# Four buffers for kept products, a second queue for finished rows and no first burst of weight differences in a decoder-layer kernel

## The chip, the core and the metric

The kernel runs on one core of a Trainium2 chip. A core has TensorE (PE, matrix products into PSUM banks), VectorE (DVE) and ScalarE (ACT) for element-wise work, GpSimd (POOL) for some element-wise work, and SyncE (SP), which here only issues transfers. Transfers between the chip's memory (HBM) and the on-chip memory (SBUF) run on 16 DMA engines; an instruction on SP, ACT or POOL asks for one, and each of these engines issues in the order of its own instructions, so a transfer that must wait holds up what stands behind it. The metric is the device time of one execution in microseconds (us); times are the median of several runs.

## The reference

One decoder layer on 2048 tokens of width 1024, in float32:

```python
hn = rms_norm(h, mix_pre_g)
proj = hn @ w_in                       # q, k, v and the input of a convolution group
attn_out = sliding_window_attention(q, k, v, attn_sinks, rel_bias)
conv_out = conformer_conv(u, conv_dw, conv_dw_b, conv_ln_g, conv_ln_b, w_conv_pw)
mixed = jnp.concatenate([attn_out, conv_out], axis=-1) @ w_out
h = h + rms_norm(mixed, mix_post_g)
hn = rms_norm(h, ffn_pre_g)
ff = (jax.nn.silu(hn @ w_gate) * (hn @ w_up)) @ w_down      # w_down: 2816 x 1024
h = h + rms_norm(ff, ffn_post_g)
```

## The kernel before

Tokens are worked on in four tiles of 512, numbered 0 to 3. Every float32 operand is split into a rounded high part and a low part (ScalarE copies the high part, `split_f` at line 840; VectorE or GpSimd subtracts, `lo` at line 844), and every product is made of three TensorE products: high by high, high by low, low by high. A matmul instruction multiplies a 128x128 block by 128x512 into one PSUM bank.

The name of a buffer in the profile is its tag, an @ and the stage: A are the input projections, B attention, C the convolution, W the output projection, H the preparation of the hidden rows for the feed-forward part, F the feed-forward products with w_gate and w_up, G the down projection with w_down. The feed-forward part takes two token tiles as one pair: tiles 0 and 1 are the first pair (stages H0, F0, G0 in the code), tiles 2 and 3 the second (H2, F2, G2). The page leaves the digits out.

For a pair, each product with w_gate and w_up is a 2x2 block product that is made with seven half-size products instead of eight, from sums and differences of the blocks of hidden rows and of the weights. The stage F has two parts.

- The early part, `stage_pre`, line 921, needs only plain blocks of hidden rows. It runs for PRE weight columns (20 for the first pair, 16 for the second). In its first half it makes the product of A11 and B11 for each of them, copies it out of its bank (line 983) and writes it to HBM (`keeps`, line 980): these are the kept results. In its second half it fetches a kept result (`fetch`, line 939, into a tile with the tag `gb`, asked for at line 943), copies it into a free PSUM bank with ScalarE (`seed`, line 955, the copy at 959) and adds the product of A12 and B21 on top. That is one block of the result, and it goes through silu (line 988) and the product of the two halves to HBM (`mids`, line 991). Weights are loaded two products at a time into `raw` (line 936).
- The main part, `stage_p1`, line 997, makes the other products. It needs sums of hidden rows, which `stage_h_sums` (line 882, operations at 893 and 904) makes while the early part runs, and fetches the kept results once more (line 1043).

A product has 12 matmuls. There are four PSUM banks for products, two buffers for `gb`, two for `at`, three for `fc`, one for `wx` and five for `chl` (`BUFS`, line 53).

The down projection (`stage_p2`, line 1163) is also made with seven products. It needs differences of the blocks of w_down; `stage_tsums` (line 1119) makes them once, during the main part of the first pair: for each of 11 groups GpSimd's queue loads four blocks (line 1126), VectorE makes four differences, and GpSimd's queue writes each to HBM (`td`, line 1138). When the four row blocks of a pair are done, `finish` (line 1141) normalises them: it reads the rows of h from `h_scr` into `chl` (line 1155), VectorE multiplies and adds, and the finished rows are written to `out` (line 1159). For the first pair this falls into the early part of the second.

The order of the work: the main line of stages is run by `run` (line 1399), and each of its yields gives so many us of estimated time to a set of lanes (`Lane`, line 1320). A lane holds stages that go on beside the main line; it earns credit at its rate, capped at 6.0, and while it has credit its next piece is emitted. A lane without work also earns. The differences of w_down are on the lane `lt` with the rate 0.2; a group costs 3.9 for its loads and 0.25 for each difference. The framework then sets the order of each engine's instructions by priorities in order of emission and by its own estimate of when an instruction could start; a difference is also tied to the newest matmul, so that it does not stand far ahead of the products.

Of the kernel before, what the change touches and what calls it, by code (L numbers as in the profile page):

```python
# [37 lines left out]
def layer_kernel(ctx, tc, x, xT, cols, rows, sinks, relb, onehot, w_in, w_pw, w_out, w_gate, w_up, w_down, out):  # L38
# [22 lines left out]
    def f2(tag, shape=(P, T)):  # L61
        return t_(tag, shape)
# [111 lines left out]
    def after_first(first, r, how="NoSync"):  # L174
        tc.add_manual_dep(
            r.ins,
            first.ins.name,
            mybir.DependencyInfo(getattr(mybir.DependencyClass, how), mybir.DependencyReason.DATA),
            reason="products of half the array stand together",
        )  # L180

    def three(o, pairs, first=True, last=True):
        n = 3 * len(pairs)
# [737 lines left out]
    def stage_pre(ws, ops, mid, keep, q0=0, q1=None):  # L921
        PRE = PRES[ws[0]]
        q1 = q1 or 2 * PRE
        L = f"F{ws[0]}"
        raws = {}
        wops = {}
        kept = {}

        def load(q):
            if q < q1 and q % 2 == 0:  # L930
                lab[0] = L
                half, m = divmod(q, PRE)
                raw = t_("raw", (P, 2, T))
                for j in range(2):
                    src, pr = MATS[m + j]
                    nc.sync.dma_start(raw[:, j], src[2 * pr][:, half * T : (half + 1) * T])
                    raws[q + j] = raw[:, j]

        def fetch(q):
            if PRE <= q < q1:  # L940
                lab[0] = L
                kept[q] = f2("gb")
                nc.sync.dma_start(kept[q], keep[q - PRE])

        def split(q):
            if q < q1:
                lab[0] = L
                raw = raws.pop(q)
                wops[q] = split_f(raw, hl("w"))
                lo(raw, wops[q], False)  # L950

        seeded = {}
        pend = []

        def seed(q):
            if PRE <= q < q1:
                lab[0] = L
                seeded[q] = mm()
                act(seeded[q], kept.pop(q), AF.Copy)  # L959

        load(q0)
        load(q0 + 2)
        for q in range(q0, q0 + 3):
            split(q)
        for q in range(q0, q1):
            half, m = divmod(q, PRE)
            started.add(f"P{ws[0]}.{q}")
            bn = "B21" if half else "B11"
            if len(ops.get(bn, ())) < 4:
                lh.until(f"{bn}.{ws[0]}")  # L970
            split(q + 3)
            load(q + 4)
            fetch(q + 2)
            lab[0] = L
            seed(q + 1)
            lab[0] = L
            o = seeded.pop(q) if half else mm()
            product(o, wops.pop(q), ops[bn], not half)
            while pend:
                nc.sync.dma_start(*pend.pop())  # L980
            if not half:
                u = f2("fa")
                act(u, o, AF.Copy)
                pend.append((keep[m], u))
            else:
                if MATS[m][0] is w_gate:
                    sg = f2("fa")
                    act(sg, o, AF.Silu)
                else:
                    vtt(sg, sg, o, ALU.mult)  # L990
                    nc.sync.dma_start(mid[0, MATS[m][1]], sg)
            yield 2.76
        while pend:
            lab[0] = L
            nc.sync.dma_start(*pend.pop())
# [123 lines left out]
    def stage_tsums(td):  # L1119
        L = "G0"  # L1120
        for pr in range(NF // 2):
# [6 lines left out]
            b11, b12, b21, b22 = b  # L1128
            for to, o, p_, q_ in ((0, b11, b12, b11), (2, b12, b22, b12), (1, b22, b22, b11), (3, b21, b21, b22)):
                lab[0] = L  # L1130
                r = vtt(o, p_, q_, ALU.subtract)
                tc.add_manual_dep(
                    r.ins,
                    made["rows"][-1].name,
                    mybir.DependencyInfo(mybir.DependencyClass.NoSync, mybir.DependencyReason.DATA),
                    reason="weight differences keep pace with the products",
                )
                nc.gpsimd.dma_start(td[to, pr], o)
                yield 0.25

    def finish(L, gb, jobs, pool=True):
        lab[0] = L
        n_ = len(jobs)
        ssq = sm(4)
        for j, (rows_, halves) in enumerate(jobs):
# [6 lines left out]
        r = rsqrt(ssq[:, 0:n_], n_, 1, pool)  # L1152
        for j, (rows_, halves) in enumerate(jobs):
            ht = f4("chl" if L == "G0" else "mid")
            nc.sync.dma_start(ht, h_scr[rows_])
            for n in range(2):
                cs = slice(n * T, (n + 1) * T)
                stt(halves[n], halves[n], r[:, j : j + 1], ht[:, cs], ALU.mult, ALU.add)
                nc.sync.dma_start(out[rows_, cs], halves[n])
            yield 2.0  # L1160
            lab[0] = L

# [304 lines left out]
    del normed[:]  # L1467
    lh.add("S0", stage_h_sums(ws, ops), lambda: "N1" in lh.done)
    run(stage_pre(ws, ops, mids[0], keeps[0], Q0))
    lt.add("TS", stage_tsums(td))  # L1470
    run(stage_p1(ws, ops, mids[0], keeps[0]))
    lt.until("TS")
# [80 lines left out]
```

## Time and profile before

| | |
|---|---|
| three runs, us | 1948.69, 1951.76, 1952.41 (median 1951.76) |
| the profiled execution: its own time, its span, us | 1951.41, 1949.7 |
| TensorE busy, us and share of the span | 1902.9, 98% |
| VectorE, ScalarE, GpSimd busy, share | 76%, 49%, 15% |
| mean granted TensorE clock | 0.993 |
| early part, first pair and second pair, us from the start, about | 498 to 650, 1286 to 1396 |
| main part, first and second pair, about | 650 to 980, 1396 to 1725 |

The profile is one execution. A line such as `PE mm@F L85 <- ACT mm@F L959: 13.6, 7, 5.1` says that TensorE stood idle before instructions of line 85 that write `mm@F`, until the ScalarE instruction of line 959 was done: 13.6 us in total, 7 times, 5.1 us the longest. In a timeline a row gives the start, the length, the engine, the line, the operation, what it writes and reads, how many in a row, and in brackets the idle time ahead and what ended it. "SPq" is SP issuing a transfer, and "DMA x<-y" is a transfer in flight. A table of stretches gives for each stretch the busy time of each engine with the number of instructions, then the mean granted clock, the share of the 16 DMA engines' time and GB/s. Line 85 is the helper that emits every matmul and line 94 the one that emits every VectorE operation, so the names of the buffers tell which stage a row belongs to.

### The profile page before, as it was taken

Reading aid. Unit: us, or ns where it says so; the run is one execution under the profiler, and the core shown is the slowest. Engines: PE = TensorE matmul, PEld = TensorE weight load, DVE = VectorE, ACT = ScalarE, POOL = GpSimd, SP = SyncE. Lnnn points to the kernel's source line nnn. Section 1 sums busy time; section 2 is a strip of 40 time slices with the busy share of each in tenths; the row PEclk is TensorE's granted clock in tenths of the full one; section 3 lists DMA queues with packets and bytes.
Section 4 is the critical chain, followed back from the end, with each engine's and each line's share of the span. In section 5 each row is a group of like instructions: output and inputs, shape, how many; then the busy total and the mean of one; then the engine's idle time right before and its main releaser. Section 6 shows DMA issues by size and latency. Waiting matters only on the chain.

```text
span 1949.7 us, 26646 instructions
## 1 busy us (share of the span) xinstructions
PE 1902.9 (98%) x8730; PEld 1537.4 (79%) x8730; DVE 1475.9 (76%) x2648; ACT 958.6 (49%) x1886; POOL 299.0 (15%) x427
## 2 busy tenths in 40 slices
PE   8999999999999999999999999998999999999997
PEld 6777777777777787788888788886788888888886
DVE  4999979995986998888579945578677776465557
ACT  5355455457658433334353555476534333345453
POOL 4011021011120111120000100000032333211003
PEclk9999999999999999999999999998999999999998
DMA  8787667667758767676477876769645443375663
GB/s 308 250 309 229 220 209 236 199 206 237 245 199 288 269 227 257 241 269 228 144 272 240 315 249 206 237 235 362 216 159 162 154 154 103 124 252 185 206 199 141
DMA packets 209578, 435.67 MB, mean 223 GB/s; under 512 B 21752, under 2 KB 39328, under 8 KB 209440
## 3 DMA queue, kind: packets, MB, share of 16 engines
q1 hardware_dynamic: 191648, 402.52, 61.8%
q0 software_dynamic: 7040, 23.07, 3.4%
q10 hardware_dynamic: 10752, 8.39, 1.3%
q8 instruction: 68, 1.11, 0.2%
q14 instruction: 70, 0.57, 0.1%
HBM read 323.26 MB, written 110.63 MB: 223 GB/s over the span
## 4 chain that ended last, share of the span: by engine, by line
PE 67%; DVE 15%; DMA 10%; issue 4%; ACT 2%; POOL 2%; SPq 1%; DVEq 0%; POOLq 0%; ACTq 0%
PE mm@F L85 30%; PE mm@G L85 17%; PE mm@A L85 8%; DVE fc@C L94 5%; PE mm@W L85 4%; PE tr@W L85 3%; PE tr@B L85 2%; DMA mids<-fa@F 2%; DVE w@F L94 1%; DMA keeps<-fa@F 1%; DVE chl@F L94 1%; DVE fa@F L94 1%; DMA w@W<-fold 1%; DMA gb@F<-keeps 1%; PE tr@B L504 1%
## 5 line engine op out<-in xcount | busy, mean ns | idle before, releaser
L94 DVE SCALAR_TENSOR_TENSOR fc@C<-glu@C,colt,fc@C 128x512 f32<-128x512 f32 x480 | 359.0, 762 | 2.7
L85 PE MATMUL mm@F<-hl@H,w@F 128*128 128x512 f32 x1056 | 261.1, 398 | 14.8 <-ACT mm@F L959 13.6
L85 PEld LDWEIGHTS mm@F<-hl@H,w@F 128*128 128x128 f32 x1056 | 201.1, 192 | 61.6 <-ACT mm@F L959 17.7
L85 PE MATMUL mm@G<-hl@G,hl@G 128*128 128x512 f32 x924 | 227.4, 393 | 1.8 <-DVE hl@G L94 1.8
L841 ACT ACTIVATE w@F<-chl@F 128x512 fp32r<-128x512 f32 x220 | 136.3, 626 | 186.3 <-PE mm@F L85 164.8
L85 PE MATMUL mm@A<-hl@A,w@A 128*128 128x512 f32 x840 | 207.9, 395 | 4.0 <-ACT w@A L127 2.1
L85 PEld LDWEIGHTS mm@G<-hl@G,hl@G 128*128 128x128 f32 x924 | 171.6, 188 | 38.3 <-DVE hl@G L94 2.6
L85 PE MATMUL mm@G<-w@G,hl@G 128*128 128x512 f32 x876 | 199.4, 389 | 0.0
L94 DVE TENSOR_TENSOR w@F<-chl@F,w@F 128x512 fp32r<-128x512 f32 x198 | 151.0, 765 | 59.9 <-ACT w@F L841 59.7
L85 PEld LDWEIGHTS mm@G<-w@G,hl@G 128*128 128x128 f32 x876 | 164.5, 188 | 34.1
L85 PEld LDWEIGHTS mm@A<-hl@A,w@A 128*128 128x128 f32 x840 | 155.2, 188 | 43.2 <-issue 3.9
L85 PE MATMUL mm@F<-mid@H,w@F 128*128 128x512 f32 x528 | 132.7, 392 | 0.8 <-DVE fa@F L94 0.8
L85 PE MATMUL mm@F<-ql@H,w@F 128*128 128x512 f32 x528 | 130.1, 391 | 0.7 <-ACT w@F L841 0.7
L85 PE MATMUL mm@F<-p@H,w@F 128*128 128x512 f32 x528 | 129.1, 389 | 0.0
L85 PE MATMUL mm@F<-x@H,w@F 128*128 128x512 f32 x528 | 125.7, 391 | 0.0
L85 PEld LDWEIGHTS mm@F<-mid@H,w@F 128*128 128x128 f32 x528 | 99.8, 189 | 22.3 <-ACT at@F L1086 1.2
L85 PEld LDWEIGHTS mm@F<-x@H,w@F 128*128 128x128 f32 x528 | 98.7, 188 | 21.3 <-issue 0.8
L85 PEld LDWEIGHTS mm@F<-p@H,w@F 128*128 128x128 f32 x528 | 99.1, 188 | 20.6
L85 PEld LDWEIGHTS mm@F<-ql@H,w@F 128*128 128x128 f32 x528 | 98.5, 188 | 21.1 <-ACT w@F L841 1.1
L507 POOL TENSOR_SCALAR_AFFINE_SELECT p@B<-p@B 128x512 f32<-128x512 f32 x62 | 56.6, 918 | 338.1 <-ACT p@B L505 336.6
L127 ACT ACTIVATE w@A<-raw@A 128x512 fp32r<-128x512 f32 x110 | 67.4, 626 | 82.4 <-PE mm@A L85 50.3
L94 DVE TENSOR_TENSOR w@G<-raw@G,w@G 128x512 fp32r<-128x512 f32 x73 | 53.6, 734 | 71.7 <-ACT w@G L841 70.7
(316 smaller groups left out, 3240.0 us busy)
## 6 DMA issues: line engine op xcount, KB each, us to landing
mids<-fa@F SPq DMA_DIRECT2D x154, 256.0 KB, 3.0
raw@A<-w_in SPq DMA_DIRECT2D x55, 512.0 KB, 4.5
w@A<-lo_in SPq DMA_DIRECT2D x84, 256.0 KB, 3.8
fc@G<-mids SPq DMA_DIRECT2D x77, 256.0 KB, 3.4
fa@G<-mids SPq DMA_DIRECT2D x75, 256.0 KB, 4.5
gb@F<-keeps SPq DMA_DIRECT2D x72, 256.0 KB, 4.0
w@W<-fold SPq DMA_DIRECT2D x32, 512.0 KB, 5.7
chl@F<-w_gate SPq DMA_DIRECT2D x22, 512.0 KB, 4.8
```

Source lines behind the costliest of these rows:

```text
L85: r = nc.tensor.matmul(*args, **kw)
L94: r = op(*args, **kw)
L127: act(w[:, 0], raw, AF.Copy)
L504: nc.tensor.transpose(o[:, i * P : (i + 1) * P], pr[:, 4 * g + i], ident)
L507: cut = nc.gpsimd.affine_select(out=pg[:, kb].rearrange("p (i q) -> p i q", q=P), in_=pg[:, 1].rearrange("p (i q) -> p i q", q=P), compare ...
L841: act(w[:, 0], x, AF.Copy)
```

## The change

It has three parts. In `stage_pre` a kept result goes by turns into a buffer of `gb` and one of `at`, two of each, and is asked for four products ahead of its use, where it was two. In `finish` the first pair (label G0) issues its reads of `h_scr` and its writes of `out` from GpSimd's queue; the second pair still uses SP's. Ahead of the stage of w_down differences the lane's saved credit, which by then is at the cap of 6.0, is set to 0. The new function `tied` holds what stood in `stage_tsums` before.

```diff
+    def tied(r):
+        tc.add_manual_dep(
+            r.ins,
+            made["rows"][-1].name,
+            mybir.DependencyInfo(mybir.DependencyClass.NoSync, mybir.DependencyReason.DATA),
+            reason="keeps pace with the products",
+        )
+        return r
...
         def fetch(q):
             if PRE <= q < q1:
                 lab[0] = L
-                kept[q] = f2("gb")
+                kept[q] = f2(("gb", "at")[q % 2])
                 nc.sync.dma_start(kept[q], keep[q - PRE])
...
             split(q + 3)
             load(q + 4)
-            fetch(q + 2)
+            fetch(q + 4)
...
-                r = vtt(o, p_, q_, ALU.subtract)
-                tc.add_manual_dep(
...
+                tied(vtt(o, p_, q_, ALU.subtract))
                 nc.gpsimd.dma_start(td[to, pr], o)
...
     def finish(L, gb, jobs, pool=True):
         lab[0] = L
+        queue = nc.gpsimd if L == "G0" else nc.sync
...
             ht = f4("chl" if L == "G0" else "mid")
-            nc.sync.dma_start(ht, h_scr[rows_])
+            queue.dma_start(ht, h_scr[rows_])
             for n in range(2):
                 cs = slice(n * T, (n + 1) * T)
                 stt(halves[n], halves[n], r[:, j : j + 1], ht[:, cs], ALU.mult, ALU.add)
-                nc.sync.dma_start(out[rows_, cs], halves[n])
+                queue.dma_start(out[rows_, cs], halves[n])
...
     run(stage_pre(ws, ops, mids[0], keeps[0], Q0))
+    lt.credit = 0.0
     lt.add("TS", stage_tsums(td))
```

The changed file is a few lines longer, so its line numbers stand 3 to 9 higher behind the first insertion (943 is now 952, 1155 is 1159, 1159 is 1163).

SP's queue in the second half of the second pair's early part, before. `gb` are kept results, `raw` weights, `out` finished rows of the first pair, `chl@H` hidden rows, `glu@G` a row of gains.

```order
L1159 DMA out<-x@G_1675_10256 128x512
L1159 DMA out<-p@G_2014_12200 128x512
L1249 DMA glu@G_2726_16614<-rows 128x512
L936 DMA raw@F_2140_12826<-w_gate 128x512
L936 DMA raw@F_2140_12826<-w_up 128x512
L888 DMA chl@H_2090_12591<-hT_116 128x2x512
L943 DMA gb@F_2129_12771<-keeps_4719 128x512
L991 DMA mids_4716<-fa@F_2118_12725 128x512
L943 DMA gb@F_2135_12797<-keeps_4719 128x512
```

The same place in the changed kernel, up to the same hidden rows (`chl@H_2090`):

```order
L1253 DMA glu@G_2725_16612<-rows 128x512
L952 DMA gb@F_2131_12775<-keeps_4719 128x512
L1253 DMA glu@G_2726_16614<-rows 128x512
L989 DMA keeps_4719<-fa@F_2115_12704 128x512
L952 DMA at@F_2137_12801<-keeps_4719 128x512
L952 DMA gb@F_2143_12833<-keeps_4719 128x512
L897 DMA chl@H_2090_12591<-hT_116 128x2x512
L945 DMA raw@F_2142_12830<-w_gate 128x512
```

The rows of `out` are gone from this queue, and three kept results, in both kinds of buffer, stand ahead of the hidden rows where before the third and fourth stood behind them.

GpSimd's queue where the rows of `finish` now stand (`chl@G` is a read of `h_scr`; in the kernel before nothing stood here between a square root of the convolution and the main part of the second pair):

```order
L1159 DMA chl@G_1974_11933<-h_scr 128x1024
L1163 DMA out<-p@G_1906_11542 128x512
L1159 DMA chl@G_1977_11949<-h_scr 128x1024
L1163 DMA out<-x@G_1834_11101 128x512
L1163 DMA out<-p@G_1906_11542 128x512
L1163 DMA out<-x@G_1834_11101 128x512
L1159 DMA chl@G_1996_12061<-h_scr 128x1024
L1163 DMA out<-p@G_1909_11561 128x512
```

Reads and writes alternate there, as they did on SP's queue.

VectorE's order in the first pair's main part, before; `wx@G` is a difference of w_down, here the first one of the second group, and `at@F` an addition that frees a PSUM bank.

```order
L94 TENSOR_TENSOR chl@F_1144_6799<-raw@F_1109_6615,chl@F_1143_6796 128x512
L94 TENSOR_TENSOR wx@G_1119_6658<-wx@G_1119_6658 128x512
L94 SCALAR_TENSOR_TENSOR fc@C_1083_6465<-glu@C_1082_6463,colt,fc@C_1083_6465 128x512
L94 TENSOR_TENSOR at@F_1115_6639<-at@F_1115_6639,mm@F_1113_6624 128x512
L94 TENSOR_TENSOR at@F_1123_6680<-at@F_1123_6680,mm@F_1114_6626 128x512
```

The same place in the changed kernel, from the same addition (`at@F_1115`) to the first difference of the first group:

```order
L94 TENSOR_TENSOR at@F_1115_6639<-at@F_1115_6639,mm@F_1113_6624 128x512
L94 TENSOR_TENSOR w@F_1137_6762<-chl@F_1108_6613,w@F_1137_6762 128x512
L94 SCALAR_TENSOR_TENSOR fc@C_1085_6469<-glu@C_1084_6467,colt,fc@C_1085_6469 128x512
L94 TENSOR_TENSOR w@F_1144_6793<-chl@F_1140_6781,w@F_1144_6793 128x512
L94 SCALAR_TENSOR_TENSOR fc@C_1085_6469<-glu@C_1084_6467,colt,fc@C_1085_6469 128x512 x2
L94 TENSOR_TENSOR w@F_1145_6818<-chl@F_1140_6781,w@F_1145_6818 128x512
L94 SCALAR_TENSOR_TENSOR fc@C_1085_6469<-glu@C_1084_6467,colt,fc@C_1085_6469 128x512
L94 TENSOR_TENSOR chl@F_1157_6913<-chl@F_1125_6677 128x512
L94 TENSOR_TENSOR wx@G_1116_6643<-wx@G_1116_6643 128x512
```

The second group of differences has moved away from these additions, and the first group now starts behind them, with convolution taps (`fc@C`) in their place.

More of the change, by code (lines that the diff above doesn't have):

```diff
@@ L1130, in stage_tsums @@
                 lab[0] = L
-                r = vtt(o, p_, q_, ALU.subtract)
-                tc.add_manual_dep(
[L1133 to L1137, printed above, removed]
+                tied(vtt(o, p_, q_, ALU.subtract))
                 nc.gpsimd.dma_start(td[to, pr], o)
```

## The prediction

> **What bounds the kernel now.** I read the list of cores, the page's busy shares, TensorE's (PE's) waits, a table of stretches, and then the timeline of the stretches in which PE's busy time falls short.
>
> ```profile
> core 0: 1949.7 us, clock 0.993
> PE 1902.9 (98%) x8730; PEld 1537.4 (79%) x8730; DVE 1475.9 (76%) x2648; ACT 958.6 (49%) x1886; POOL 299.0 (15%) x427
> ...
> PE mm@F L85 <- ACT mm@F L959: 13.6, 7, 5.1
> PE mm@F L85 <- DVE at@F L94: 3.7, 2, 2.3
> ...
> PE mm@F L85 <- DVE fa@F L94: 0.8, 1, 0.8
> ```
>
> PE is the bound: it is idle for 1949.7 - 1902.9 = 46.8 us. Whatever the change does must show as less of that idle time, or as matmuls that run faster. The largest wait by far, 13.6 us in 7 pieces, is for line 959, the ScalarE copy that puts a kept result into a PSUM bank. The columns of the next table are PE, PEld, DVE, ACT and POOL busy, granted clock, DMA share, GB/s.
>
> ```profile
> 660.00:700.00 40.00, 37.71 (x159) 30.71 (x158) 36.91 (x60) 12.78 (x23) 8.05 (x15) 0.96 0.66 222
> ...
> 1285.00:1310.00 25.00, 25.00 (x115) 20.71 (x114) 20.60 (x48) 20.20 (x39) 0.00 (x0) 1.00 0.79 269
> 1310.00:1335.00 25.00, 25.00 (x125) 20.88 (x124) 18.52 (x51) 21.08 (x49) 0.00 (x0) 1.00 0.94 324
> 1335.00:1360.00 25.00, 17.25 (x56) 12.73 (x55) 23.30 (x49) 13.25 (x24) 0.00 (x0) 0.80 1.03 376
> 1360.00:1385.00 25.00, 20.70 (x82) 15.94 (x81) 19.19 (x31) 14.85 (x27) 0.00 (x0) 0.93 0.79 267
> 1385.00:1420.00 35.00, 35.00 (x156) 29.00 (x155) 18.58 (x25) 14.45 (x26) 2.82 (x2) 1.00 0.54 178
> ```
>
> The bad stretch is 1335 to 1385 us, in the second pair's early part: PE loses 7.75 + 4.30 us and part of its clock. The DMA engines are full in its first half (1.03), VectorE (DVE) is 93% busy there, GpSimd (POOL) is idle; after 1385 all have room. PE's timeline:
>
> ```profile
> 1330.33 2.88 PE L85 MATMUL mm@F<-ql@H,w@F 128*128 128x512 f32 x12
> 1333.05 5.38 PE L85 MATMUL mm@F<-hl@H,w@F 128*128 128x512 f32 x23
> 1341.07 7.57 PE L85 MATMUL mm@F<-hl@H,w@F 128*128 128x512 f32 x24 [2.65 <-ACT mm@F L959]
> 1353.74 8.43 PE L85 MATMUL mm@F<-hl@H,w@F 128*128 128x512 f32 x24 [5.10 <-ACT mm@F L959]
> 1363.38 3.04 PE L85 MATMUL mm@F<-hl@H,w@F 128*128 128x512 f32 x12 [1.21 <-ACT mm@F L959]
> 1367.55 3.04 PE L85 MATMUL mm@F<-hl@H,w@F 128*128 128x512 f32 x12 [1.13 <-ACT mm@F L959]
> 1372.55 17.77 PE L85 MATMUL mm@F<-hl@H,w@F 128*128 128x512 f32 x70 [1.96 <-ACT mm@F L959]
> ```
>
> Undisturbed, 12 matmuls take 1333.05 - 1330.33 = 2.72 us, 0.227 each. From 1341.07 - 2.65 = 1338.42 to 1372.55, 34.1 us, PE did 24 + 24 + 12 + 12 = 72 of them, worth 16.3 us. The loss is 17.8 us: 2.65 + 5.10 + 1.21 + 1.13 + 1.96 = 12.05 of gaps, and the rest slow matmuls behind gaps (24 took 7.57 and 8.43 where 2.88 + 2.72 = 5.6 is their pace). What the copies wait for, from 1318 to 1385 us:
>
> ```profile
> ACT mm@F L959 <- DMA gb@F<-keeps: 7.0, 4, 3.0
> ...
> 1346.41 6.60 DMA gb@F<-keeps
> ...
> SPq L1159 <- DVE p@G L94: 6.5, 4, 3.5
> ...
> SPq L943 <- ACT mm@F L959: 4.8, 5, 2.0
> ```
>
> ScalarE stands 7.0 us for kept results still in flight (one took 6.60 us). The queue that asks for them (SP) stands 4.8 us until an earlier copy frees one of the two buffers, and 6.5 us in front of finished rows (line 1159) that VectorE has not written yet; all later requests are behind those. Two products are 24 matmuls, 5.44 us, less than one such transfer.
>
> **The change, part by part.** *Four buffers, asked four ahead.* No instruction is added. In the second pair, four results cover 10.9 us, longer than the 6.60. The bounds of what that returns are 0 and 17.8 us. Neither end is right: the stretch also has work that does not shrink. DVE's busy time from 1285 to 1385 is 20.60 + 18.52 + 23.30 + 19.19 = 81.6 us; at the 93% that DVE shows where it is pressed hardest (23.30 of 25) that takes 87.6 us, where a full recovery leaves 82.2. I keep 5.4 us of the loss and take a gain of 12.4. The DMA engines give nearly the same: 0.79 + 0.94 + 1.03 + 0.79 times 25 is 88.8 us, which takes 86.2 at 1.03. The two buffers lent by the tag `at` are next wanted by additions of the main part, after the last kept result is copied: 0. What needs this stretch next, the second pair's main part, does not hold it back:
>
> ```profile
> 1373.77 0.68 DVE L94 TENSOR_TENSOR mb@H<-chl@H,mb@H 128x512 fp32r<-128x512 f32 x1
> ...
> L85 PE MATMUL mm@F<-mid@H,w@F x48: 389/389/390, 1396.0 to 1437.1; 128*128 128x512 f32 x48
> ```
>
> The sums of the second pair's hidden rows end at 1374.5 and are first multiplied at 1396.0: some 21 us of slack, more than the 12.4.
>
> In the first pair the same copies cost little:
>
> ```profile
> 600.02 3.93 PE L85 MATMUL mm@F<-hl@H,w@F 128*128 128x512 f32 x16 [0.72 <-ACT mm@F L959]
> ...
> 627.85 25.11 PE L85 MATMUL mm@F<-hl@H,w@F 128*128 128x512 f32 x108 [0.83 <-ACT mm@F L959]
> ```
>
> 0.72 + 0.83 = 1.55 us; bounds 0 and 1.6, taken 1.5, since the four-deep buffers act there alike.
>
> *Finished rows through GpSimd's queue.* Eight reads of h_scr and 16 writes of out leave SP and go to POOL.
>
> ```profile
> out<-x@G SPq DMA_DIRECT2D x16, 256.0 KB, 2.2
> ...
> chl@G<-h_scr SPq DMA_DIRECT2D x12, 512.0 KB, 5.3
> wx@G<-w_down POOLq DMA_DIRECT2D x22, 256.0 KB, 4.2
> ...
> L1138 POOL DMA_DIRECT2D td<-wx@G x22: 539/544/547, 658.1 to 896.4; - x22
> ```
>
> On POOL an issue costs 0.544 us: 24 of them 13.1 us, on an engine with 0.00 busy in the four stretches from 1285 to 1385; nothing else stands behind them in POOL's order until the main part of the second pair. I cost it at 0, covered by that idle time; were the cover gone, 13.1 us of POOL would still lie beside PE. SP loses 24 issues and the 6.5 us of waits; that gain is inside the 12.4, not a second one. Who waits for a late read is VectorE (its group of finishing operations from 1285 to 1385):
>
> ```profile
> L94 DVE SCALAR_TENSOR_TENSOR p@G<-p@G,sm@G,chl@G 128x512 f32<-128x512 f32 x8 | 6.0, 749 | 6.1 <-DMA chl@G<-h_scr 6.0
> ```
>
> 6.0 us for eight reads today. Bounds for the move: 6.0 us better (SP's blockages gone), or as much worse as the last rival says; I take 0: a 256 KB transfer on POOL's queue lands in 4.2 us and one on SP's in 2.2, so the flight itself does not get shorter, while the blockages that it escapes are worth about as much.
>
> *No burst of w_down differences.* The stage no longer starts with saved-up credit, so its second group does not follow the first at once.
>
> ```profile
> 667.54 2.88 PE L85 MATMUL mm@F<-ql@H,w@F 128*128 128x512 f32 x12
> 672.71 2.36 PE L85 MATMUL mm@F<-yt@H,w@F 128*128 128x512 f32 x6 [2.29 <-DVE at@F L94]
> 674.86 2.45 PE L85 MATMUL mm@F<-mid@H,w@F 128*128 128x512 f32 x6
> ...
> 670.70 0.69 DVE L94 TENSOR_TENSOR wx@G<-wx@G 128x512 f32<-128x512 f32 x1 [1.72 <-DMA wx@G<-w_down]
> ...
> 671.97 1.28 DVE L94 TENSOR_TENSOR at@F<-at@F,mm@F 128x512 f32<-128x512 f32 x2
> ```
>
> DVE, in order, stands 1.72 us before the second group's first difference for its w_down load, with the additions (at@F) that free PE's banks behind it. PE loses 2.29 us, and the 12 matmuls behind it take 677.3 - 672.7 = 4.6 instead of 2.88 us: 4.0 together. Bounds 0 and 4.8 (with the 0.8 us for fa@F). I take 4.0: the new order has both additions ahead of any difference. The 44 differences are as many as before and end some 30 us later (6 units of credit at a rate of 0.2), in stretches where DVE has room:
>
> ```profile
> 850.00:900.00 50.00, 50.00 (x222) 41.39 (x221) 44.58 (x72) 20.69 (x37) 9.72 (x18) 1.00 0.75 253
> 900.00:950.00 50.00, 50.00 (x224) 41.38 (x223) 37.23 (x60) 17.51 (x31) 0.54 (x1) 1.00 0.54 169
> ```
>
> ```profile
> L1138 POOL DMA_DIRECT2D td<-fc@G x22: 539/540/547, 663.1 to 902.5; - x22
> ...
> L1186 SPq DMA_DIRECT2D mb@G<-td x44: 319/376/1747, 1047.9 to 1216.1; - x44
> ```
>
> The last difference leaves at 902.5 and the first is read at 1047.9, so the delay costs 0; without the room it would come back as waits like the 2.29.
>
> **A rule of the clock.** After gaps of 2.29, 2.65 and 5.10 us the matmuls behind them lost 1.7, 2.0 and 2.8 us. [...] The trace shows the shorter gaps costing clock too (0.96 granted around the 2.29), so I go by its rows.
>
> **Sum.** 12.4 + 1.5 + 0 + 4.0 = 17.9 us off 1951.4, the profiled execution's own time (0.4 us under the median of the three runs, 1951.76): 1933.5 us. The runs shown spread over 3.7 us, 0.19%, so a difference within 0.2% (3.9 us) is no difference.
>
> **Rivals.** *Another wait takes its place (smaller gain).* The stretch keeps its transfers. If they go no faster than the 0.94 of 1310 to 1335, 88.8 us of them need 94.4 of the 100 us: a gain of 5.6 instead of 12.4, 1940.3 us; with the first pair's terms halved too, 1943. For it: the share of 1.03. Against: 0.54 right behind the stretch, into which what is not urgent can slip. Chance 0.24.
>
> *More comes back.* All of 17.8 + 1.5 + 4.8, and other small waits that the re-ordered VectorE drops, at most 3.3 us: 27.4, down to 1924. Chance 0.06.
>
> *Nothing arrives.* The kept results come in time, but the weight loads, on the same full DMA engines, hold the same products, and what the burst cost comes back among the later differences: the gain is 0, 1951.4 us. Against: SP loses 24 issues ahead of those loads. Chance 0.08.
>
> *Slower: late rows through GpSimd.* In POOL's order a read of h_scr stands behind writes of out that wait for VectorE, so a read may start only when its use is next. Then VectorE, in order, stands a whole landing (5.3 us) for each of eight reads, 42.4 us instead of 6.0, with the weight splits for PE behind it. VectorE has 100 - 81.6 - 6.0 = 12.4 us of other idle time there; 24.0 us fall on PE: 1951.4 - 17.9 + 24.0 = 1957.5 us. It decides from 4.5 us per read on. Against: SP's order had the same neighbours and cost 6.0. [...] Chance 0.10.
>
> **Chances.** Forecast 0.52, smaller gain 0.24, more 0.06: faster 0.82; same 0.08; slower 0.10. The likeliest alone reaches from 1928 to 1940. The range 1925 to 1948 takes in the first rivals and leaves out the slower one, most of "nothing arrives" and the far end of "more".
>
> **What would show it.** Right: PE's waits for the kept results' copies fall from 13.6 to under 4 us in all; in the 50 us in which the second pair's second half begins PE is busy over 46 us, at a clock over 0.97; no PE wait over 1 us for at@F around 672 us; SP no longer waits for p@G. Wrong: VectorE waits over 20 us for h_scr rows, or ScalarE waits for raw loads where it waited for kept ones, or the waits for at@F grow between 750 and 950 us.

## The result, and the profile after

The change makes the kernel faster. It was measured beside the kernel before on three occasions; the last two are the runs e8_after and e12_after further down.

| occasion | before, median us (runs) | after, median us (runs) | ratio, 95% interval | gain by the ratio |
|---|---|---|---|---|
| first | 1950.70 (4) | 1940.52 (4) | 0.9947, 0.993 to 0.9964 | 10.3 us |
| second | 1954.39 (11) | 1937.46 (4) | 0.9908, 0.9895 to 0.9921 | 18.0 us |
| third | 1953.03 (11) | 1936.39 (5) | 0.9918, 0.9904 to 0.9932 | 16.0 us |

The kernel before spreads more than the changed one (1948.5 to 1963.3 us over all its 55 runs, against 1935.1 to 1941.7 over 13), and the intervals of the first two occasions do not overlap: the gain is between some 10 and 18 us. The profiled execution of the changed kernel took 1939.15 us. Its row in the list of cores:

```profile
core 0: 1937.4 us, clock 0.996
```

TensorE's waits, as far as they concern the feed-forward part:

```profile
PE mm@F L85 <- ACT w@F L850: 4.0, 2, 3.1
...
PE mm@F L85 <- DVE at@F L94: 2.7, 2, 1.8
...
PE mm@F L85 <- ACT mm@F L968: 1.7, 3, 1.2
...
PE mm@F L85 <- DVE w@F L94: 1.5, 2, 1.1
```

Line 968 is the copy of a kept result (959 before): 13.6 us of waits became 1.7. In its place stand 4.0 + 1.5 us for weight splits (w@F), which cost 0.7 us before, in the first pair. The stretches of the second pair's early part, and the one around 672 us (columns as before: PE, PEld, DVE, ACT, POOL busy, clock, DMA share, GB/s):

```profile
1285.00:1310.00 25.00, 25.00 (x118) 20.73 (x117) 19.65 (x47) 21.30 (x41) 2.20 (x4) 1.00 0.87 308
1310.00:1335.00 25.00, 25.00 (x122) 20.95 (x121) 22.13 (x62) 21.34 (x49) 7.41 (x14) 1.00 0.93 327
1335.00:1360.00 25.00, 23.10 (x100) 18.16 (x98) 20.97 (x41) 15.78 (x30) 3.33 (x7) 1.00 1.04 401
1360.00:1385.00 25.00, 21.43 (x85) 16.33 (x84) 19.28 (x32) 13.68 (x26) 0.00 (x0) 0.93 0.87 308
1385.00:1420.00 35.00, 35.00 (x156) 28.99 (x155) 25.16 (x34) 15.36 (x27) 8.77 (x6) 1.00 0.52 162
660.00:700.00 40.00, 40.00 (x178) 33.14 (x177) 38.70 (x63) 16.50 (x29) 4.85 (x9) 1.00 0.55 192
```

From 1335 to 1385 TensorE now works 44.5 us of 50 instead of 38.0, at clocks of 1.00 and 0.93 instead of 0.80 and 0.93. The DMA engines are as full as they were in the first half (1.04, where it was 1.03) and fuller in the second (0.87, where it was 0.79). Around 672 us nothing is left of the gap. TensorE's timeline in the bad stretch:

```profile
1331.39 22.17 PE L85 MATMUL mm@F<-hl@H,w@F 128*128 128x512 f32 x97
1354.63 3.28 PE L85 MATMUL mm@F<-hl@H,w@F 128*128 128x512 f32 x12 [1.07 <-DVE w@F L94]
1358.74 7.99 PE L85 MATMUL mm@F<-hl@H,w@F 128*128 128x512 f32 x34 [0.83 <-ACT w@F L850]
1369.87 13.03 PE L85 MATMUL mm@F<-hl@H,w@F 128*128 128x512 f32 x48 [3.14 <-ACT w@F L850]
1382.74 0.61 PE L85 MATMUL mm@F<-mid@H,w@F 128*128 128x512 f32 x2
```

97 matmuls run without a gap where four gaps stood; the main part begins at 1382.7 instead of 1396.0. What is late instead stands in VectorE's timeline:

```profile
1340.48 0.69 DVE L94 TENSOR_TENSOR chl@H<-mid@G,chl@H 128x512 f32<-128x512 f32 x1 [3.96 <-DMA chl@H<-hT]
```

the flights of the hidden rows in this stretch (`chl@H`, from issue to landing):

```profile
DMA to landing us min/median/max: 5.7/6.7/12.1
```

and two of the waits from 1318 to 1385 us that the prediction spoke of, VectorE's and SP's:

```profile
DVE p@G L94 <- DMA chl@G<-h_scr: 0.8, 1, 0.8
...
SPq L952 <- ACT mm@F L968: 0.6, 3, 0.2
```

One load of hidden rows took 12.1 us (longest before: 7.1). VectorE stands 3.96 us for it, and then has all the sums, low parts and finished rows of that time to do at once. SP waits 0.6 us for a free buffer where it waited 4.8, and not at all for finished rows (p@G). VectorE waits 0.8 us for a row of h where it waited 3.1.

The gain by stages, from the positions at which TensorE begins them (first pair's feed-forward, first pair's down projection, second pair's feed-forward, second pair's down projection; the first pair's down projection ends where its last matmul begins, and the last stage with the span), by TensorE's groups before and then after:

```profile
L85 PE MATMUL mm@G<-hl@G,hl@G x924: 387/389/505, 981.3 to 1285.4; 128*128 128x512 f32 x185
L85 PE MATMUL mm@G<-w@G,hl@G x876: 388/389/390, 1725.2 to 1934.4; 128*128 128x512 f32 x176
...
L85 PE MATMUL mm@F<-x@H,w@F x528: 387/389/504, 498.5 to 1724.5; 128*128 128x512 f32 x176
```

```profile
L85 PE MATMUL mm@G<-hl@G,hl@G x924: 387/389/504, 978.9 to 1283.8; 128*128 128x512 f32 x185
L85 PE MATMUL mm@G<-w@G,hl@G x876: 389/389/389, 1712.7 to 1921.9; 128*128 128x512 f32 x176
...
L85 PE MATMUL mm@F<-x@H,w@F x528: 387/389/504, 500.5 to 1712.0; 128*128 128x512 f32 x176
```

| stage | before, us | after, us | gain |
|---|---|---|---|
| to the first pair's feed-forward part | 498.5 | 500.5 | -2.0 |
| first pair's feed-forward part | 482.8 | 478.4 | 4.4 |
| first pair's down projection | 304.1 | 304.9 | -0.8 |
| second pair's feed-forward part | 439.8 | 428.9 | 10.9 |
| second pair's down projection | 224.5 | 224.7 | -0.2 |
| sum | 1949.7 | 1937.4 | 12.3 |

Up to 498 us the instructions of both kernels stand in the same order on every engine, so those 2.0 us are a difference between two executions, not the change. In the two later profiles of the changed kernel the first pair's feed-forward part took 478.2 and 475.3 us and the second pair's 427.8 and 431.4: the two parts together gain 15.3, 16.6 and 15.9 us in the three profiles, each set against the one profile of the kernel before.

### The profile page after: what moved, and what is told of

It is laid out like the page before. It is cut to its first block, busy times and chain, and to the rows that moved or that the text cites. A ratio compares the mean times of both kernels' runs of the same rounds, so it can differ in the third digit from the quotient of the medians.

```text
span 1937.4 us, 26679 instructions
## 1 busy us (share of the span) xinstructions
PE 1897.0 (98%) x8730; PEld 1532.9 (79%) x8730; DVE 1475.7 (76%) x2648; ACT 959.2 (50%) x1886; POOL 310.2 (16%) x451
## 4 chain that ended last, share of the span: by engine, by line
PE 66%; DVE 15%; DMA 12%; issue 3%; ACT 2%; POOL 2%; SPq 0%; DVEq 0%; ACTq 0%; POOLq 0%
PE mm@F L85 30%; PE mm@G L85 17%; PE mm@A L85 8%; DVE fc@C L94 5%; PE mm@W L85 4%; PE tr@W L85 3%; PE tr@B L85 2%; DMA mids<-fa@F 2%; DMA chl@H<-hT 1%; DMA fc@G<-w_down 1%; DMA raw@A<-w_in 1%; DVE w@F L94 1%; DVE fa@F L94 1%; DVE chl@F L94 1%; DMA mixT<-yt@C 1%
## 5 line engine op out<-in xcount | busy, mean ns | idle before, releaser
L85 PE MATMUL mm@F<-hl@H,w@F 128*128 128x512 f32 x1056 | 256.8, 393 | 7.2 <-ACT w@F L850 4.0
```

What stands on the lines that cost most here:

```text
L85: r = nc.tensor.matmul(*args, **kw)
```

## The experiments

Two questions were asked: which of the three parts brings the gain, and what holds the second pair's early part now. For the second there were two theories. A: VectorE is the limit of that stretch (the prediction kept 5.4 us of the loss for this). B: the bytes on the 16 DMA engines are.

| run | what it is | ratio to before, 95% | second pair's feed-forward part, us |
|---|---|---|---|
| e1_four | first part alone | 0.9933, 0.9919 to 0.9947 | 430.4 |
| e2_queue | second part alone | 1.0010, 0.9996 to 1.0024 | 440.4 |
| e3_noburst | third part alone | 0.9974, 0.9964 to 0.9984 | 439.3 |
| e7, e11 | first and third part, two runs | 0.9923, 0.9910 to 0.9937; 0.9926, 0.9913 to 0.9939 | 432.6; 430.8 |
| e8, e12 | the whole change again | 0.9908; 0.9918 | 427.8; 431.4 |
| e4_pool_lo | whole, low parts of sums on GpSimd | 0.9966, 0.9953 to 0.9979 | 439.0 |
| e5_nostt | whole, without the multiply-adds of finishing | 0.9934, 0.9921 to 0.9947 | 432.7 |
| e10_small_stt | whole, those multiply-adds on 8 columns | 0.9943, 0.9927 to 0.9959 | 430.2 |
| e6_noout | whole, first pair's finished rows hardly written | 0.9879, 0.9862 to 0.9895 | 420.0 |
| e9_early_odd | whole, half of the finishing moved earlier | 0.9903, 0.9889 to 0.9917 | 427.5 |

e8, e7, e5 and e6 ran on one occasion, e12, e11, e10 and e9 on another; runs of one occasion are compared with each other. e1 to e4 ran on a fourth, with the kernel before but without the changed kernel beside them, so they are set against the changed kernel by ratios only. The last column is worked out as in the table of stages, from each run's profile.

### The parts alone

e1_four:

```diff
-                kept[q] = f2("gb")
+                kept[q] = f2(("gb", "at")[q % 2])
-            fetch(q + 2)
+            fetch(q + 4)
```

> The kernel before with the first part alone: four buffers, kept results asked for four products ahead; finished rows stay on SP, the burst stays. Theory 1 (the buffers do it: 10.9 us of cover against a flight of 6.6): 8 to 12 us faster than before, TensorE's waits for the kept results' copies fall from 13.6 us to under 4. Rival (SP's queue is the cause: its 6.5 us of waits in front of finished rows hold the requests back, however many buffers there are): under 5 us faster, and those waits stay over 6 us.

e2_queue:

```diff
+        queue = nc.gpsimd if L == "G0" else nc.sync
-            nc.sync.dma_start(ht, h_scr[rows_])
+            queue.dma_start(ht, h_scr[rows_])
-                nc.sync.dma_start(out[rows_, cs], halves[n])
+                queue.dma_start(out[rows_, cs], halves[n])
```

> The kernel before with the second part alone: the first pair's finished rows on GpSimd's queue. Theory 1: two buffers cover 5.44 us, less than the flight, so at most 3 us faster than before and TensorE still waits over 8 us for the kept results' copies. Rival (SP's queue is the cause): 5 us or more faster. The rival that late rows of h_scr hold VectorE: slower than before, VectorE's waits for them over 20 us.

e3_noburst:

```diff
+    lt.credit = 0.0
     lt.add("TS", stage_tsums(td))
```

> The kernel before with the third part alone: no saved credit ahead of the differences of w_down. Theory 1: 4.0 us faster than before, as the prediction has it, and no TensorE wait for at@F around 672 us. Rival (the wait comes back among the later differences): within 1.5 us of before, with waits for at@F that grow by 2 us or more between 700 and 980 us.

The buffers alone bring 13.1 us (10.4 to 15.8, by the ratio), a little more than the 8 to 12 expected and nearly as much as the whole change, which brought 14.8 as a mean of its three occasions. The queue alone brings nothing (1.0010). No burst alone brings 5.1 us (3.1 to 7.0). TensorE's waits for kept results, in the profile of e1_four and then in that of e2_queue:

```profile
PE mm@F L85 <- ACT w@F L841: 7.5, 3, 4.5
...
PE mm@F L85 <- ACT mm@F L959: 1.6, 2, 1.3
```

```profile
PE mm@F L85 <- ACT mm@F L959: 15.2, 5, 6.0
```

With four buffers those waits are nearly gone although finished rows still stand in SP's queue (ten writes of line 1159 in e1_four between 1313 and 1344 us); with the queue freed and two buffers they are all there. From 1284 to 1400 us TensorE waits 12.1, 12.7 and 13.2 us for kept results in the three kernels with two buffers (before, e2, e3), and between 0 and 1.6 us in the six profiles with four buffers that move and leave out nothing (the changed kernel three times, e1, e7, e11). So SP's blockages were not what made the kept results late; the depth was. The same weight splits (w@F) come up in e1_four: they are no effect of GpSimd's queue.

The 5.1 us of the third part are not found where the prediction placed them. In the profile of e3_noburst the gap around 672 us is gone (of TensorE's two waits for at@F from 640 to 980 us, 2.2 us in all, the one of 2.0 falls behind 860 us, where it is busy 107.79 of 110 us), but the first pair's feed-forward part takes 482.6 us, as before (482.8): kept results cost it 3.3 us of waits where they cost 1.5, and that addition (at@F) another 2.0. In e1_four, which keeps the burst, the gap is gone as well (from 490 to 980 us TensorE waits for no at@F of VectorE's): in its order both additions stand ahead of the second group's first difference. So leaving out the burst does remove the gap, but another order does too, and how much the third part adds beside the buffers is not shown.

### The second part in company

e7_four_noburst and e11_four_noburst are one kernel, the change without its second part; e8_after and e12_after are the changed kernel beside it.

> The kernel before with the first and the third part, without the second: finished rows stay on SP's queue. Theory 1 (the queue part is worth nothing once there are four buffers): within 2 us of the changed kernel. Rival (GpSimd's queue costs something there): 3 us or more faster than the changed kernel, up to 0.991 of the kernel before.

> The changed kernel once more, on the same chip as the next three, so that they can be set beside it. By its first runs 0.9947 of the kernel before (0.993 to 0.9964). If the four buffers and the burst were simply added (0.9933 and 0.9974 alone), 0.991.

> The change without its second part (finished rows on SP) a second time; the first time it was 2.7 us behind the changed kernel with intervals that overlapped. Prediction's value (the queue costs and brings 0): within 1.5 us of the changed kernel beside it. Rival (with four buffers in use SP's queue is worth freeing): 2 to 4 us slower again.

> The changed kernel a third time, to be set beside the next three. The first two comparisons gave 0.9947 and 0.9908 of the kernel before. If the kernel before simply spreads more than the changed one from chip to chip, this lies between them, 1935 to 1942 us, with the changed kernel's own runs within 3 us of each other.

Without the second part the medians are 2.7 us (e7 against e8) and 3.6 us (e11 against e12) higher, where within 2 and then within 1.5 us had been expected; the second lies in its rival's 2 to 4. By the ratios it is 0.15% and 0.08%, and the intervals overlap both times. Both differences point the same way and neither is clear of the scatter, so whether the queue part is worth something beside four buffers stays undecided. The two other parts added up (0.9933 x 0.9974 = 0.9907) are measured together as 0.9923 and 0.9926: a part of what each brings alone is the same idle time (the gap at 672 us is gone in both) or comes back, or it is the scatter; the intervals do not decide it. The ratio of e12_after lies between the first two, as expected, but its five runs spread over 6.5 us, where 3 had been expected.

### VectorE or the DMA engines

e4_pool_lo:

```diff
-                lo(x, o, False)
+                lo(x, o, bool(ws[0]))
```

> The changed kernel with the low parts of the second pair's sums of hidden rows (16 subtractions) moved from VectorE to GpSimd. After the change TensorE waits 5.5 us for weight splits (w@F) at 1354 to 1385 us, where VectorE is busy 13.96 of 14 us. Theory A (VectorE is the new limit of that stretch): 16 x 0.60 = 9.6 us less of its time there, the waits for w@F fall under 2 us, and the time is 4 to 8 us under the changed kernel's 1940.5. Rival B (the 16 DMA engines are the limit: share 1.04 there): within 1.5 us of the changed kernel, with waits for raw loads or kept results in place of w@F. Rival C (GpSimd's slower subtractions hold the chl buffers, so hidden rows and h_scr rows come later): slower than the changed kernel, VectorE waiting more than the 4.0 us for chl@H.

It brings less than the whole change did on any occasion, and its second pair's part takes 439.0 us, as if nothing had been changed. That it is slower is what its rival C said, but not by C's mechanism: VectorE waits 2.6 us for hidden rows (chl@H), not more than 4.0. It does not test theory A, since it does not take time off VectorE. Its timelines of VectorE and then of GpSimd:

```profile
1342.11 1.25 DVE L94 TENSOR_TENSOR sm@G<-sm@G 128x2 f32<-128x2 f32 x1
...
1345.52 0.75 DVE L94 SCALAR_TENSOR_TENSOR p@G<-p@G,sm@G,chl@G 128x512 f32<-128x512 f32 x1
1346.18 2.15 DVE L94 SCALAR_TENSOR_TENSOR x@G<-x@G,sm@G,chl@G 128x512 f32<-128x512 f32 x1
```

```profile
1341.61 1.74 POOL L854 TENSOR_TENSOR x@H<-chl@H,x@H 128x512 fp32r<-128x512 f32 x1
...
1346.48 1.29 POOL L854 TENSOR_TENSOR yt@H<-chl@H,yt@H 128x512 fp32r<-128x512 f32 x1
```

A multiply-add of 0.75 us takes 2.15 beside a subtraction on GpSimd, and an addition on two columns (sm@G), 0.15 to 0.17 us elsewhere, takes 1.25. So 16 subtractions of 0.60 us, from start to start, were exchanged for 16 of 1.3 to 1.7 us, with longer rows of VectorE beside them; by what mechanism was not shown.

e5_nostt takes work off VectorE, and e10_small_stt does it again with every instruction kept. The scheduler sets the order anew each time: in e5_nostt 33 of VectorE's instructions, beside the 16 left out, and 29 of ScalarE's stand elsewhere than in the changed kernel; in e10_small_stt it is 32 of VectorE's 2,648 and 17 of ScalarE's 1,918, all of them after 1300 us.

```diff
+                if L == "G0":
+                    queue.dma_start(out[rows_, cs], ht[:, cs])
+                    continue
                 stt(halves[n], halves[n], r[:, j : j + 1], ht[:, cs], ALU.mult, ALU.add)
```

> The changed kernel without the 16 multiply-adds on VectorE that finish the first pair's rows (left out: those rows of the output are the rows of h alone; reads, writes and their queue stay). Theory A (VectorE is the new limit between 1335 and 1385 us): 16 x 0.66 = 10.6 us less of its time in the early part, waits of TensorE for w@F fall from 5.5 us to under 2, and the time is 4 to 8 us under the changed kernel's. Rival B (the DMA engines are the limit): within 2 us of the changed kernel, and the waits stay.

```diff
-                stt(halves[n], halves[n], r[:, j : j + 1], ht[:, cs], ALU.mult, ALU.add)
+                w_ = 8 if L == "G0" else T
+                stt(halves[n][:, 0:w_], halves[n][:, 0:w_], r[:, j : j + 1], ht[:, n * T : n * T + w_], ALU.mult, ALU.add)
```

> The changed kernel with the 16 multiply-adds that finish the first pair's rows done on 8 of their 512 columns (left out: the other columns of those rows stay unfinished). Every transfer stays as large as it is and VectorE has some 10 us less to do in the second pair's early part. Theory B (the DMA engines are what limits the rest of that stretch): within 2 us of the changed kernel, TensorE's waits for w@F stay over 3 us. Theory A (VectorE does): 4 to 8 us faster, those waits gone.

e6_noout takes bytes off the DMA engines and leaves VectorE its work; its order differs from the changed kernel's by 42 of VectorE's instructions and 22 of ScalarE's, more than that of e10_small_stt.

```diff
+                if L == "G0":
+                    queue.dma_start(out[rows_.start : rows_.start + 1, cs], halves[n][0:1])
+                    continue
                 queue.dma_start(out[rows_, cs], halves[n])
```

> The changed kernel, of each of the first pair's 16 writes of finished rows only one row in 128 (left out: the other rows of that half of the output). This takes 4 MB off the DMA engines in the second pair's early part, of some 28, and leaves VectorE's work as it is. Rival B (the DMA engines are the limit, hidden rows and weights come late): VectorE's wait of 4.0 us for chl@H goes, the waits for w@F fall under 2 us, 4 to 8 us faster than the changed kernel. Theory A: under 2 us faster.

Less work for VectorE brought nothing: e5_nostt and e10_small_stt are both slower than the changed kernel beside them, by 0.26 and 0.25 points, with intervals that touch or overlap a little. By the medians it is 4.8 and 7.1 us, neither theory's number (A said 4 to 8 us faster, B within 2). The six runs of e10_small_stt spread from 1937.6 to 1947.3 us, and the profiled one, 1937.92, is the second fastest of them. TensorE's waits for w@F are 8.1 us in e5_nostt and 2.7 in e10_small_stt, where B said over 3; e10_small_stt has 4.9 us for kept results beside them.

Fewer bytes brought 4.8 us (1937.46 to 1932.64; the intervals of the ratios only touch, at 0.9895). The stretches of e10_small_stt, then of the changed kernel in e8_after, then of e6_noout, and TensorE's timeline in e6_noout:

```profile
1334.00:1359.00 25.00, 20.06 (x88) 15.95 (x87) 17.23 (x28) 13.89 (x26) 1.51 (x3) 1.00 1.04 399
1359.00:1384.00 25.00, 22.32 (x92) 17.70 (x91) 21.12 (x34) 15.62 (x29) 1.01 (x1) 0.93 0.82 280
```

```profile
1309.00:1334.00 25.00, 25.00 (x122) 20.95 (x122) 21.27 (x59) 22.28 (x51) 6.43 (x13) 1.00 0.94 327
1334.00:1359.00 25.00, 23.56 (x103) 18.79 (x103) 22.48 (x44) 15.99 (x29) 4.30 (x8) 1.00 1.04 402
```

```profile
1309.00:1334.00 25.00, 25.00 (x126) 20.95 (x126) 20.38 (x52) 22.71 (x53) 6.18 (x12) 1.00 0.81 280
1334.00:1359.00 25.00, 25.00 (x112) 20.71 (x111) 24.96 (x56) 18.16 (x35) 3.88 (x8) 1.00 1.05 396
1359.00:1384.00 25.00, 25.00 (x112) 20.68 (x111) 24.83 (x41) 16.64 (x31) 2.77 (x1) 1.00 0.86 295
```

```profile
1333.42 43.91 PE L85 MATMUL mm@F<-hl@H,w@F 128*128 128x512 f32 x193
```

In e6_noout TensorE runs the second half of the early part without one gap, 193 matmuls in a row, while VectorE is busy 24.96 and 24.83 us of 25: a full VectorE does not by itself hold TensorE up. In e10_small_stt VectorE has room (17.23 of 25), and TensorE loses 4.94 us all the same. Theory A falls. Theory B fits: with the 4 MB of writes gone, the share from 1309 to 1334 is 0.81 where it was 0.94; the longest flight of hidden rows is 7.9 us where it was 10.5 in e8_after, and VectorE waits for none of them where it waited 2.4 us.

But the order changed with the bytes, and order is a third candidate that no run separates from them. No transfer stands in the chain of the longest gap of the changed kernel, the 3.14 us before 1369.87 above. VectorE's rows there, and then ScalarE's:

```profile
1366.83 0.69 DVE L94 TENSOR_TENSOR fa@F<-fa@F,mm@F 128x512 f32<-128x512 f32 x1 [1.82 <-ACT mm@F L968]
1367.43 0.69 DVE L94 TENSOR_TENSOR chl@H<-chl@H,chl@H 128x512 f32<-128x512 f32 x1
```

```profile
1368.15 0.63 ACT L913 ACTIVATE mb@H<-chl@H 128x512 fp32r<-128x512 f32 x1 [1.45 <-DVE chl@H L94]
...
1369.21 1.14 ACT L850 ACTIVATE w@F<-raw@F 128x512 fp32r<-128x512 f32 x2
```

VectorE stands idle before a product of results (fa@F), which begins 0.1 us after TensorE's last matmuls before the gap end (1366.73). Behind it in VectorE's order stands a sum of hidden rows (chl@H), ScalarE stands for that sum, and the weight split that TensorE needs (w@F) comes behind in ScalarE's order. The gap of 3.14 us and the waits of 1.82 and 1.45 us are the same in all three profiles of the changed kernel, though VectorE waited 4.0, 2.4 and 6.0 us for hidden rows in them. In e6_noout that sum stands two such products earlier. So e6_noout shows that the bytes or the order were the limit; which of them stays open. Why e5_nostt and e10_small_stt are slower than the changed kernel, and not equal to it, was not settled.

The last experiment moves the same 4 MB instead of leaving them out. The squares of `finish` wrote their unused result into the buffer `junk`, which put them in order behind the squares of the last token tile; they now write it to `vtok`, which is free by then, and the odd half reads h_scr into `wx`, free as well:

```diff
-    def finish(L, gb, jobs, pool=True):
+    def finish(L, gb, jobs, pool=True, odd=False):
...
-                act(junk[:, 0:T], halves[n], AF.Square, scale=D**-0.5, accum_out=ssq[:, 2 * n + j : 2 * n + j + 1])
+                act(vtok[:, 0:4].rearrange("p a b -> p (a b)") if L == "G0" else junk[:, 0:T], halves[n], AF.Square, scale=D**-0.5, accum_out=ssq[:, 2 * n + j : 2 * n + j + 1])
...
-            ht = f4("chl" if L == "G0" else "mid")
+            ht = f4("mid" if L != "G0" else "wx" if odd else "chl")
...
-                        (rows_of(j, 1), (home("c21", "p", j), home("p7", "x", j))) for j in (b - 1, b)], last))
+                        (rows_of(j, 1), (home("c21", "p", j), home("p7", "x", j))) for j in (b - 1, b)], last, True))
```

> The changed kernel with half of the first pair's finishing moved ahead of the second pair's early part, nothing left out: the squares of the first pair write their unused result to another buffer, so that they no longer stand in order behind those of the last token tile, and the odd half reads h_scr into the free buffer wx in place of chl. 4 reads of 512 KB and 8 writes of 256 KB, 4 MB in all, then lie before 1284 us, where the DMA engines' share is 0.44 to 0.64. Theory B: 3 to 6 us faster than the changed kernel, waits of TensorE for w@F under 3 us in all. Rival: the transfers come back as other waits in the down projection, within 1.5 us of the changed kernel.

It is 0.9 us faster than the changed kernel beside it (1935.53 against 1936.39), 0.15 points by the ratio, with overlapping intervals: theory B's 3 to 6 us did not come. The time is the rival's, within 1.5 us, but the new waits are not in the down projection, where it put them. The second pair's part takes 427.5 us, against 431.4 in e12_after and 427.8 in e8_after. TensorE's waits from 1284 to 1409 us, and the stretches there:

```profile
PE mm@F L85 <- ACT mm@F L968: 2.6, 1, 2.6
PE tr@H L845 <- ACT chl@W L822: 1.5, 1, 1.5
```

```profile
1309.00:1334.00 25.00, 23.40 (x117) 18.52 (x116) 10.71 (x28) 18.02 (x30) 1.62 (x3) 1.00 0.95 331
1334.00:1359.00 25.00, 22.43 (x92) 17.98 (x91) 18.04 (x30) 17.66 (x34) 2.70 (x5) 0.93 0.98 327
1359.00:1384.00 25.00, 25.00 (x112) 20.68 (x111) 24.96 (x42) 17.63 (x33) 2.95 (x1) 1.00 0.95 347
```

The waits for w@F are gone, as theory B has it. But the share does not fall (0.95, 0.98, 0.95), presumably since what was asked for later takes the room, and two other things are late, a kept result (2.6 us) and the last tile's normalised rows (chl@W, 1.5 us here). Those come from sums that VectorE now makes behind the finishing moved ahead of them, for whose rows of h it waits 5.8 us; that this is the cause was not tested. So taking 4 MB away paid, with another order beside it; moving 4 MB by some 50 us did not measurably pay, and new waits stand there instead.

## Why the prediction was right, and where it was not

The forecast was 17.9 us off 1951.4, 1933.5 us. The gain is 10.3 us on the first occasion and 18.0 and 16.0 on the others, and the times, 1936.4 to 1940.5, lie 3 to 7 us over the forecast and inside its range. By the profiles the two feed-forward parts gain 15.3 to 16.6 us. How near each occasion came is in part luck: the first time, 1940.5, lies just outside the 1928 to 1940 that the prediction gave to its likeliest case, and on the 1940.3 of its rival, and part of the larger gain of the later two is a slower kernel before (1954.4 and 1953.0 us against 1950.7).

- **Four buffers, 12.4 us: mechanism right, size a little high, and the reason for what is kept wrong.** The waits for kept results went, as the depth against the flight had it, and e1_four and e2_queue show that the depth does it alone. The second pair's part gained 10.9 us in the profile (12.0 and 8.4 in the two later ones). The mis-sized term is the 5.4 us that the prediction kept of the loss: with e6_noout as the stretch without loss (420.0 us), the change leaves 428.9 - 420.0 = 8.9 us, and 7.8 and 11.4 in the later profiles, of 439.8 - 420.0 = 19.8 before (17.8 in the prediction). It took the 5.4 from VectorE at 93%. In e6_noout VectorE is at over 99% with no loss at all, so the amount of VectorE's work was not the reason. What the runs leave is the bytes on the DMA engines, which the prediction named second, or the order of VectorE's and ScalarE's work, which it did not name. One reading beside the term is off: SP's 6.5 us in front of finished rows belong to 1280 to 1400 us; from 1318 to 1385 us, where the prediction puts them, they are 1.8. No term of the sum uses them.
- **First pair's kept results, 1.5 us: wrong.** 1.5 us of waits were there and 1.7 are there after (1.3 in each of the two later profiles). ScalarE's waits for these transfers did go there, from 5.1 us to none between 590 and 655 us, but TensorE's waits for its copies stayed, so something else made those copies late. The deeper buffers do not act alike in both pairs.
- **Finished rows on GpSimd, 0: right alone, undecided beside the buffers.** e2_queue gives 1.0010; beside four buffers the part is 2.7 and 3.6 us by the medians, within the scatter. In the profile of the changed kernel the issues took 0.53 to 0.58 us, and GpSimd had the time (12.9 us busy from 1285 to 1385 us).
- **No burst, 4.0 us: place right, size not shown.** The gap and its slow matmuls are gone from 660 to 760 us. Alone it brings 5.1 us (3.1 to 7.0), but not in the first pair's part (482.6 us in e3_noburst), and in e1_four the gap goes with the burst still there. Some came back: the waits for at@F between 750 and 980 us are 2.7 + 0.5 us (with fa@F) where 1.4 stood.

Of its signs of being right, one is missing: TensorE busy over 46 of the 50 us, at a clock over 0.97, where the second half begins; it is 44.5, at 1.00 and 0.93. That is the rival "another wait takes its place": it gave 1940.3 us by transfers that go no faster, and its mechanism (the share stays at 1.04, weight splits wait in place of kept results) is there beside the forecast's. "Nothing arrives" fell with the ratio. The slower rival, late rows of h_scr through GpSimd, fell by its own number: VectorE's waits for them went down, from 6.0 us to 1.9. One sign of being wrong did show in the first profile: the waits for at@F between 750 and 950 us grew from 1.4 to 2.7 us. In e8_after and e12_after they are at most 1.5 and 0.4. The slow matmuls behind gaps are in the forecast as the rows gave them, 5.8 us of the 17.8 and 1.7 of the 4.0; what the runs show of the clock stands at the end.

## What to carry to other kernels

Set depth times the time of one step against the flight while the DMA engines are full: here two buffers of 2.72 us each, 5.44 us, were too few against flights up to 6.8 us, and four, 10.9 us, were enough against flights up to 10.7 us and one of 13.5 (first profile of the changed kernel); three were not tried. Once such a wait is gone, ask which resource was full beside it: a busy engine that nobody waits for is no limit (VectorE in e6_noout, 24.96 us of 25 without a gap of TensorE), and the plainest test is to take away its work, or the transfers, and see whether the idle time goes. Taking work away also lets the scheduler re-order the engines, so compare the orders before you name the limit. An output that nobody reads can still set an order, when many instructions share one buffer for it.

## What the runs showed of the hardware

In these traces the clock behind a gap of TensorE was half for some us or not lowered at all, and the length of the gap did not decide it. In the kernel before it was 0.50 for the 3 us from 673.5, 1342.5 and 1373.5 us, behind gaps of 2.29, 2.65 and 1.96 us, and for the 6 us from 1353, 0.7 us before the gap of 5.10 us ends; from 1359.5 to 1372, with gaps of 1.21 and 1.13 us, it was 1.00. The same gap of TensorE, 3.14 us before the same 48 matmuls, in the first profile of the changed kernel and then in e8_after (stretches of 2 to 3 us; the number in brackets behind PE is matmuls):

```profile
1369.00:1371.00 2.00, 1.13 (x4) 0.60 (x4) 2.00 (x4) 2.00 (x5) 0.00 (x0) 0.96 0.86 281
1371.00:1374.00 3.00, 3.00 (x8) 2.25 (x8) 2.96 (x6) 0.90 (x2) 0.00 (x0) 0.50 0.59 197
1374.00:1376.00 2.00, 2.00 (x10) 1.62 (x9) 1.46 (x3) 0.76 (x2) 0.00 (x0) 0.93 0.81 254
```

```profile
1369.00:1371.00 2.00, 1.86 (x7) 1.11 (x8) 2.00 (x5) 2.00 (x5) 0.00 (x0) 1.00 0.91 313
1371.00:1374.00 3.00, 3.00 (x15) 2.45 (x14) 2.96 (x6) 1.07 (x3) 0.00 (x0) 1.00 0.70 208
```

In the one the clock is 0.50 for the 3 us that begin about 1 us after the matmuls resume, and 8 matmuls run where 15 run in the other. In e12_after the 3.14 us cost the clock again (0.50 from 1371 to 1374). In e9_early_odd a gap of 2.57 us brought the same half clock (0.51 from 1350 to 1353), in e10_small_stt one of 3.25 us did not (1.00 from 1359 to 1364). Among these, gaps of 1.96 to 2.65 us and the one of 5.10 had the half clock, the one of 3.25 us had not, and the one of 3.14 us had it in two profiles of three; what decides it was not shown.
